# Fox half of the merge inside the front, y splits in the place of u, probabilities divided on ScalarE: a change to a hybrid RWKV-7 and forgetting-attention layer

## The chip, the cores and the metric

The kernel runs on one core of one Trainium2 chip. The metric is the device time of one execution in microseconds (us); the median of several executions stands for a kernel. The engines are named as the profile names them: PE (TensorE matmul), PEld (TensorE weight load), DVE (VectorE), ACT (ScalarE), POOL (GpSimd), SP (SyncE, which issues the DMAs).

## What is computed

One layer over 512 tokens and 16 learned ones put before them (528 rows, 1024 channels). In the reference, cut to what matters:

```python
u = rmsnorm(h, norm_mix)
proj = u @ w_in                              # 1024 -> 1792 (rw) + 1544 (fx) + 2048 (gates)
gates = sigmoid(proj[..., C_RW + C_FX:] + b_gate)
y_rw = rwkv7_branch(feat_rw, ...)            # 8 heads of 64: S = S*w + (S a) b + v k ; y = S r ; group norm, bonus, gate
y_fx = fox_branch(feat_fx, ...)              # 8 heads of 64: causal attention, blocks of 128 queries
#   logits = q.k * scale + F_q - F_k,  F = cumsum(log_sigmoid(f));  p = softmax(mask(logits));  p @ v
merged = gates[..., :1024] * (y_rw @ w_out_rw) + gates[..., 1024:] * (y_fx @ w_out_fx)
h = h + merged @ w_o
z = rmsnorm(h, norm_mlp)
h = h + square(relu(z @ w_up)) @ w_down      # 1024 -> 4096 -> 1024
return h[16:]
```

All is float32. A wide matmul is done in three passes: each operand x is split into `hi` (x cast to the narrower format `fp32r`) and `lo = x - hi`, and `hi*hi + hi*lo + lo*hi` is accumulated. The small matmuls of attention and of the recurrence are done on plain float32.

## The kernel before

**The front.** u is made once, with channels on the partitions, as `uhi` and `ulo` in a pool `up`. The input projection runs in 42 blocks of 128 output columns. The first two (for the low-rank decays and the gate) are made while u is made. The other 40 are jobs in a list sorted by rank (`ask`): 12 of Fox attention (rank 2), 12 of the recurrence (rank 1), 16 of the gates (rank 9). The stream `projections` takes them one by one: `fetch` loads two 256 KB pieces of weights, `convert` splits them (cast on ACT, subtraction on POOL, tiles `wraw`, `whi`, `wlo` with four buffers each), and 48 matmuls follow (L500), in two halves of 264 columns, or for gates in one of 512. A gate block is then copied to `gt` by ACT (L520) and written to DRAM as `gates_d[i]`.

Beside it run other streams. `fox_features` normalises q and k and turns v for the four pairs of heads. `attention` makes, for each pair and each of four query blocks, the scores of both heads (`scored`), their transposes (`turned`) and the product with v (`mixed`). `recurrent` makes for each of four pairs of heads the chunk matrices of the RWKV-7 branch (nine chunks of 64: L826 in `scores`), inverts them for two pairs at once (`inverse`), and starts `chain`, nine dependent steps (L964, L970, L982 and on) through which the state goes; after four chunks each, `group_norm` norms the outputs, turns them and writes `y_rw`.

**What sets the order.** TensorE's instructions stand in the order in which the Python streams are advanced. `Turns.run` always advances the stream of the lowest rank whose next step a planner (`Clock`, a model of each engine's times) holds for ready within the `ROOM` of its rank; a stream can also wait for an `Event`. The other engines' instructions are put in order by a scheduler with priorities, which each stream's rank raises (`AHEAD`).

In `scored` the subtraction of the keys' F and the running minimum are one DVE operation over PSUM and the broadcast row `along[e]` (that is -F of the keys); the causal mask comes in by a matmul of the identity with `masks` into the last 128 columns. ACT takes the exponential with its row sum, DVE the reciprocal `rsum`. In `mixed` the transposed probabilities are the weights and 64 columns of v move (L666 for the 16 learned tokens, L668 for the blocks); ACT scales the result by `rsum` into `yn`, TensorE turns it (L674), ACT copies it into `y_fx`.

**The merge.** When all streams are done, y_rw and y_fx are split into `yhi`, `ylo` (L283, L284). Then come eight output blocks m, for each of them two loads of a piece of weights and, for each branch br, 12 matmuls (L1104) beside this work on a gate tile `gl`, of which each branch has two buffers:

```python
nc.sync.dma_start(g, gates_d[8 * br + m])
G.tensor_tensor(g, g, rs[:, NM:], ALU.mult)                       # L1098, POOL
act(g, g, AF.Tanh, bias=..., scale=0.5)                           # L1099, ACT
V.scalar_tensor_tensor(g, g, 1.0, po, ALU.add, ALU.mult)          # L1106, DVE
...
G.tensor_tensor(pp[0], pp[0], pp[1], ALU.add)                     # L1108, POOL
merged = act(mhi[:, m, :], pp[0], AF.Copy, scale=0.5)             # L1109
V.scalar_tensor_tensor(mlo[:, m, :], pp[0], 0.5, mhi..., ...)     # L1110
```

**The rest.** The output projection runs in two halves (L1136 and L1153), into PSUM banks of the pool that the merge uses too. Then come the second norm, its transposes (L1169) into `zhi`, `zlo`, and the MLP (L1187, L1220). `hres` holds x, loaded behind the merge's loads.

Of the kernel before, what the change touches and what calls it, by code (L numbers as in the profile page):

```python
# [27 lines left out]
CDEC = math.exp(-0.5)  # L28

# [154 lines left out]
class Turns:  # L184
# [5 lines left out]
    ROOM = {0: 0.0, 1: 1.0, 2: 1.5, 3: 1.0, 4: 2.5, 8: 0.5}  # L190
# [32 lines left out]
def kernel(ctx, tc, ht, x, win, par, cst, gain, lora, wout, wo, wup, wdn, out, dbg=None):  # L223
# [16 lines left out]
    masks = cp.tile([128, 2, 128], BF16, name="masks")  # L240
# [55 lines left out]

    with ExitStack() as st:
        up = st.enter_context(tc.tile_pool(name="up", bufs=1))
# [8 lines left out]
        uhi = up.tile([128, KB, T], F32R, name="uhi")  # L307
        ulo = up.tile([128, KB, T], F32R, name="ulo")
# [37 lines left out]
        with tc.tile_pool(name="xp", bufs=2) as xp:  # L346
# [9 lines left out]
            for j in range(2):  # L356
                for i, blk in enumerate((B_LORA, B_GD)):
                    w2[i].append(load_h(win[blk][:, 512 * j:512 * j + 512], V, "w", (4, 4, 4)))
                load_x(0, 1 + j)
# [4 lines left out]
            cmask = xp.tile([128, 128], F32, name="cmask", bufs=1)  # L364
# [35 lines left out]
            V.tensor_copy(masks[:, 0, :], ident)  # L400
            V.tensor_copy(masks[:, 1, :], cmask)
# [36 lines left out]
        for t_ in (lhi, llo):  # L438
            ck.w[t_.tensor.name] = [(0, 128, 0, 2 * T, 14.0)]
# [8 lines left out]
        asked = [0]  # L448

# [8 lines left out]
        def fetch(job):  # L458
            raws = []
            for j in range(2):  # L460
                raw = wp.tile([128, 512], F32, name="wraw", bufs=4)
# [4 lines left out]
        def convert(job, raws):  # L466
            w = []
            for raw in raws:
                hi = wp.tile([128, 512], F32R, name="whi", bufs=4)
                lo = wp.tile([128, 512], F32R, name="wlo", bufs=4)  # L470
# [5 lines left out]
        def projections(total):  # L476
            fetched, done = None, 0
            while done < total:
# [5 lines left out]
                while cur is not None:  # L484
# [29 lines left out]
                    cur = nxt  # L514

        def gate_job(i):
            def begin():
                def evac(po, sl):
                    gt = wp.tile([128, S], F32, name="gt", tag="wraw", bufs=4)
                    A.copy(gt, po)  # L520
                    nc.sync.dma_start(gates_d[i], gt)
# [4 lines left out]
        fox_ready = [Event() for i in range(4)]  # L526
        fox_done = [Event() for i in range(4)]
        fox_tiles = {}

        def fox_features():  # L530
            for p in range(4):
                b0 = B_PAIR + 6 * p
                if p > 1:
                    yield fox_done[p - 2]

                def ask_normed(blk, parts, name):
# [15 lines left out]
                    d["in"] = ask(2, blk, begin, parts)  # L552
# [21 lines left out]
                def begin():  # L574
# [6 lines left out]
                    return evac  # L581
                q = yield from normed(dq, SEQ, qg8)
                v_in = ask(2, b0 + 2, begin)
# [18 lines left out]
        def attention():  # L602
            pTm = fp.tile([128, 2, 128], F32, name="pTm")
            G.memset(pTm, 0.0)
            for p in range(4):
# [10 lines left out]
                def scored(i):  # L616

                    n = NM + 128 * (i + 1)
                    parts = [(0, n)] if n <= 512 else [(0, n - 256), (n - 256, n)]
                    yield lambda: max(ck.ready(q, k), banks(2 * len(parts)))  # L620
                    scs = [[], []]
                    for a, b in parts:
                        for e, hs in enumerate(hss):
                            sc = psm("psc")[:, :b - a]
                            mm(sc, q[hs, 128 * i:128 * i + 128], k[hs, a:b], start=True, stop=b < n)
                            scs[e].append((sc, a, b))
                    for e in range(2):
                        mm(scs[e][-1][0][:, b - a - 128:], masks[:, 0, :], masks[:, 1, :], start=False, stop=True)
                    pes, sums = [], []
                    for e in range(2):  # L630
# [9 lines left out]
                        V.reciprocal(rsum, rsum)  # L640
                        pes.append(pe)
                        sums.append(rsum)
                    return pes, sums
# [18 lines left out]
                def mixed(i, pTs, sums):  # L662
                    yield lambda: max(ck.ready(vt, vm, *pTs[0], *pTs[1], *sums), banks(1))
                    py = psm("py")[:, :128]
                    for e, hs in enumerate(hss):
                        mm(py[:, hs], pTs[e][1], vm[:, hs], start=True, stop=False)  # L666
                        for j in range(i + 1):
                            mm(py[:, hs], pTs[e][0][:, j, :], vt[:, j, hs], start=False, stop=j == i)  # L668
                    yn = fp.tile([128, 128], F32, name="yn")
# [633 lines left out]
```

## Time and profile before

| | |
|---|---|
| median of three executions | 930.76 us (929.88 to 933.67) |
| profiled execution: time, and span in the trace | 930.17 us, 928.4 us |
| busy PE, PEld | 883.4 us (95%), 724.3 us (78%) |
| busy DVE, ACT, POOL | 455.9, 446.7, 194.3 us |
| granted TensorE clock, mean | 0.987 |
| moved by DMA | 107.87 MB, mean 116 GB/s |

A busy time is the sum over an engine's instructions in the profiled execution; the engines run beside each other, so that the shares add up to more than the span. "L500" is line 500 of the kernel. In a group's row stand line, engine, operation, output and inputs, the count, then total busy time and the mean of one in ns; behind a further bar is the engine's idle time just before and what ended most of it. `a <- b: t, n, m` in the list of waits says that a's engine stood idle for t us in n waits that b ended, m the longest. A row of the chain that ended last has the start in us, the duration and the operation.

### The profile page before, as it was taken

The page shows a single profiled execution, that of the slowest core. Times are in us where ns is not written, and L with a number is a line of the kernel's source. Part 1 is how long each engine was busy: PE and PEld are TensorE (multiplying, and loading weights), DVE is VectorE, ACT ScalarE, POOL GpSimd, SP SyncE. Part 2 cuts the span into 40 slices and gives each one's busy share as a digit, 9 for nine tenths or more (in the row PEclk, how much of TensorE's full clock was granted, in tenths as well). Part 3 has the DMA queues.
Part 4 walks back from the last instruction along what each step waited for, and adds up shares of the span by engine and source line. Part 5 has one row for each costly group of instructions (what it writes and reads, how often), then busy time and mean ns, then how long its engine had stood idle before and what let it go on. Part 6 is the DMA issues. An engine that isn't in the chain of part 4 may idle for free.

```text
span 928.4 us, 15700 instructions
## 1 busy us (share of the span) xinstructions
PE 883.4 (95%) x6016; PEld 724.3 (78%) x6016; DVE 455.9 (49%) x850; ACT 446.7 (48%) x933; POOL 194.3 (21%) x170
## 2 busy tenths in 40 slices
PE   7899998998999989999989799999999999999998
PEld 6778876985788777867767578988888888888886
DVE  6574747346538653224675755344423244543322
ACT  7758646364666553555564453344322234442221
POOL 1463733324106442212055400000000000000000
PEclk9999999999999999999999899999999999999999
DMA  5245353225653543444374550132333333332331
GB/s 207 72 118 157 100 132 119 92 70 147 173 171 92 134 133 101 118 141 128 101 234 146 173 175 1 49 100 93 100 92 102 95 98 101 92 103 91 123 116 56
DMA packets 86235, 107.87 MB, mean 116 GB/s; under 512 B 21128, under 2 KB 41864, under 8 KB 86160
## 3 DMA queue, kind: packets, MB, share of 16 engines
q1 hardware_dynamic: 86160, 106.87, 37.9%
q8 instruction: 47, 0.77, 0.3%
q14 instruction: 28, 0.23, 0.1%
HBM read 88.87 MB, written 17.97 MB: 115 GB/s over the span
## 4 chain that ended last, share of the span: by engine, by line
PE 43%; POOL 2%; DVE 2%; DMA 2%; issue 1%; ACT 0%; POOLq 0%; DVEq 0%
PE po L1187 19%; PE pd L1220 19%; PE po L1136 2%; PE po L1153 2%; DMA gl<-gd 2%; POOL gl L1108 1%; POOL gl L1098 1%; DVE ylo L284 1%; PE pd L1169 0%; DVE mlo L1110 0%; DVE gl L1106 0%; ACT mhi L1109 0%; DVE we L284 0%; ACT gl L1099 0%; PE po L1104 0%
## 5 line engine op out<-in xcount | busy, mean ns | idle before, releaser
L260 DVE TENSOR_TENSOR wlo<-wraw,whi 128x512 fp32r<-128x512 f32 x152 | 108.4, 715 | 179.4 <-ACT whi L259 177.9
L259 ACT CAST whi<-wraw 128x512 fp32r<-128x512 f32 x152 | 93.9, 620 | 192.9 <-PE pd L1220 109.6
L500 PE MATMUL pj<-uhi,whi 128*128 128x264 f32 (+1 forms) x480 | 167.2, 348 | 3.0 <-ACT vf L579 2.8
L472 POOL TENSOR_TENSOR wlo<-wraw,whi 128x512 fp32r<-128x512 f32 x80 | 111.7, 1402 | 220.1 <-ACT whi L471 191.6
L500 PE MATMUL pj<-uhi,wlo 128*128 128x264 f32 (+1 forms) x480 | 155.6, 324 | 0.0
L500 PE MATMUL pj<-ulo,whi 128*128 128x264 f32 (+1 forms) x480 | 155.2, 323 | 0.0
L500 PEld LDWEIGHTS pj<-uhi,whi 128*128 128x128 f32 x480 | 91.5, 191 | 17.6 <-issue 5.5
L1220 PE MATMUL pd<-whi,fhi 128*128 128x512 f32 x256 | 99.6, 389 | 0.0
L1220 PE MATMUL pd<-wlo,fhi 128*128 128x512 f32 x256 | 99.6, 389 | 0.0
L1220 PE MATMUL pd<-whi,flo 128*128 128x512 f32 x256 | 99.6, 389 | 0.0
L500 PEld LDWEIGHTS pj<-uhi,wlo 128*128 128x128 f32 x480 | 91.2, 190 | 7.5 <-POOL wlo L472 0.2
L1187 PE MATMUL po<-zhi,whi 128*128 128x512 f32 (+1 forms) x248 | 94.8, 382 | 0.0
L1187 PE MATMUL po<-zlo,whi 128*128 128x512 f32 (+1 forms) x248 | 94.8, 382 | 0.0
L1187 PE MATMUL po<-zhi,wlo 128*128 128x512 f32 (+1 forms) x248 | 94.8, 382 | 0.0
L500 PEld LDWEIGHTS pj<-ulo,whi 128*128 128x128 f32 x480 | 91.7, 191 | 4.0
L471 ACT CAST whi<-wraw 128x512 fp32r<-128x512 f32 x80 | 48.9, 617 | 23.8 <-PE pj L500 13.3
L1220 PEld LDWEIGHTS pd<-wlo,fhi 128*128 128x128 f32 x256 | 48.1, 188 | 10.0
L1220 PEld LDWEIGHTS pd<-whi,flo 128*128 128x128 f32 x256 | 48.1, 188 | 9.9
L1220 PEld LDWEIGHTS pd<-whi,fhi 128*128 128x128 f32 x256 | 48.1, 188 | 9.9
L1187 PEld LDWEIGHTS po<-zhi,wlo 128*128 128x128 f32 x248 | 46.6, 188 | 9.1
L1187 PEld LDWEIGHTS po<-zlo,whi 128*128 128x128 f32 x248 | 46.6, 188 | 9.0
L1187 PEld LDWEIGHTS po<-zhi,whi 128*128 128x128 f32 x248 | 46.6, 188 | 8.9
(307 smaller groups left out, 1487.1 us busy)
## 6 DMA issues: line engine op xcount, KB each, us to landing
wraw<-in_win SPq DMA_DIRECT2D x84, 256.0 KB, 2.9
wraw<-in_wup SPq DMA_DIRECT2D x64, 256.0 KB, 2.6
wraw<-in_wdn SPq DMA_DIRECT2D x64, 256.0 KB, 2.6
rec<-rec SPq DMA_DIRECT2D x36, 256.0 KB, 2.9
gd<-gt SPq DMA_DIRECT2D x16, 256.0 KB, 2.1
wraw<-in_wout SPq DMA_DIRECT2D x16, 256.0 KB, 3.1
gl<-gd SPq DMA_DIRECT2D x16, 256.0 KB, 3.0
wraw<-in_wo SPq DMA_DIRECT2D x16, 256.0 KB, 2.9
```

The costliest lines, as they stand in the source:

```text
L259: A.copy(hi, raw)
L260: low.tensor_tensor(lo, raw, hi.bitcast(F32), ALU.subtract)
L284: V.tensor_tensor(lo, x, hi.bitcast(F32), ALU.subtract)
L471: A.copy(hi, raw)
L472: G.tensor_tensor(lo, raw, hi.bitcast(F32), ALU.subtract)
L500: mm(po, a, b[:, k, a0:a1], start=n == 0, stop=n == 23)
L1098: G.tensor_tensor(g, g, rs[:, NM:], ALU.mult)
L1108: G.tensor_tensor(pp[0], pp[0], pp[1], ALU.add)
L1136: mm(pd[i], a[:, k, 128 * i:128 * i + 128], b, start=k == 0 and n == 0, stop=k == 7 and n == 2)
L1153: mm(po, a[:, k, 128 * i:128 * i + 128], b[:, k, :], start=n == 0, stop=n == 23)
L1187: mm(po[:, t0:t1], a, b[:, k, t0:t1], start=n == 0, stop=n == 23)
L1220: mm(pd[i], a[:, b_, 128 * i:128 * i + 128], b, start=b_ == 0 and n == 0, stop=b_ == 15 and n == 2)
```

## The change

- **Attention.** The mask is added to the last 128 columns in use of `along[e]` by POOL, where before a matmul put it into PSUM; the query blocks go 3, 2, 1, 0, since a masked column of a block is not used by the earlier ones. ACT divides the probabilities by their sum ahead of the transposes. In the product v is the weight, the probabilities move, and the result comes out turned: the two heads use the two halves of the array's columns by turns, and the scaling and the transpose of the result are gone.
- **Gates.** The multiplication of a gate block by `rs` goes from the merge to the front (POOL, before the write to DRAM).
- **The merge.** The pool `up` stays open; y's splits take the tags and memory of `uhi` and `ulo` (and later z's do), so they are made when the last projection has read u. A new stream `fox_merged` makes y_fx's splits, the eight Fox blocks of the merge with their gates, and writes the gated products back to `gates_d[8 + m]`. `rw_split` makes y_rw's splits. The loop behind the front then has only the rw blocks, and loads two tiles for each m, the gate and the gated Fox product.
- **Weights.** `wraw` has five buffers, `whi` and `wlo` have six.
- **The recurrence.** The M matrices are made in tiles `Mt` of three chunks, from which six DMAs each time (four to `rec_d`, two into `M`) take what is kept; the two heads share one tile `M`. The bonus is made in place. A pair's keys and values are asked for by events, the inverse is a stream of its own, and the streams' ranks and `ROOM` are others: recurrent 1, attention 2, Fox features 3, where attention was 1, Fox features 2, recurrent 3.

```diff
-    ROOM = {0: 0.0, 1: 1.0, 2: 1.5, 3: 1.0, 4: 2.5, 8: 0.5}
+    ROOM = {0: 0.0, 1: 1.0, 2: 1.0, 3: 1.5, 4: 2.5, 5: 0.0, 6: 0.0, 8: 0.5}
...
-        return [load_h(src[:, 512 * j:512 * j + 512], low[j], "w", (4, 4, 4)) for j in range(2)]
+        return [load_h(src[:, 512 * j:512 * j + 512], low[j], "w", (WR, WH, WH)) for j in range(2)]
...
-                    gt = wp.tile([128, S], F32, name="gt", tag="wraw", bufs=4)
+                    gt = wp.tile([128, S], F32, name="gt", tag="wraw", bufs=WR)
                     A.copy(gt, po)
-                    nc.sync.dma_start(gates_d[i], gt)
+                    def finish():
+                        G.tensor_tensor(gt, gt, rs[:, NM:], ALU.mult)
+                        nc.sync.dma_start(gates_d[i], gt)
+                    return finish
...
+                    for e in range(2):
+                        G.tensor_tensor(along[e][:, n - 128:n], along[e][:, n - 128:n], cmask, ALU.add)
                     yield lambda: max(ck.ready(q, k), banks(2 * len(parts)))
...
-                    for e in range(2):
-                        mm(scs[e][-1][0][:, b - a - 128:], masks[:, 0, :], masks[:, 1, :], start=False, stop=True)
...
                         V.reciprocal(rsum, rsum)
+                        act(pe[:, :n], pe[:, :n], AF.Copy, scale=rsum)
...
-                        mm(py[:, hs], pTs[e][1], vm[:, hs], start=True, stop=False)
-                        for j in range(i + 1):
-                            mm(py[:, hs], pTs[e][0][:, j, :], vt[:, j, hs], start=False, stop=j == i)
-                    yn = fp.tile([128, 128], F32, name="yn")
-                    for e, hs in enumerate(hss):
-                        act(yn[:, hs], py[:, hs], AF.Copy, scale=sums[e])
-                    ...
-                    nc.tensor.transpose(pyT, yn, ident)
-                    A.copy(y_fx[:, p, 128 * i:128 * i + 128], pyT)
+                        mm(py[hs], vm[:, hs], pTs[e][1], start=True, stop=False)
+                    for j in range(i + 1):
+                        for e, hs in enumerate(hss):
+                            mm(py[hs], vt[:, j, hs], pTs[e][0][:, j, :], start=False, stop=j == i)
+                    A.copy(y_fx[:, p, 128 * i:128 * i + 128], py)
...
-                for i in range(4):
+                for i in (3, 2, 1, 0):
...
-                    for e in range(2):
-                        V.tensor_tensor(M[e][:, c0:c0 + 3, :], sps[e][:, :3, :], bc(tmask, 1, 3), ALU.mult)
-                for e, hs in enumerate(hss):
-                    self.save(hss[1 - e], 128 * e, 128 * e + 128, M[e][hss[1 - e]])
-                    self.save(hs, 384, 448, M[e][hs, :, 64:])
+                    for e, hs in enumerate(hss):
+                        Mt = rp.tile([128, 3, 128], F32, name="Mt", bufs=4)
+                        V.tensor_tensor(Mt, sps[e][:, :3, :], bc(tmask, 1, 3), ALU.mult)
+                        nc.sync.dma_start(self.M[hs, c0:c0 + 3, :], Mt[hs, :, :64])
+                        self.save(hss[1 - e], 128 * e, 128 * e + 128, Mt[hss[1 - e]], c0)
+                        self.save(hs, 384, 448, Mt[hs, :, 64:], c0)
...
+        def part(k, c0, c1):
+            split(merge[0][:, k, c0:c1], merge[1][:, k, c0:c1], (y_rw, y_fx)[k // 4][:, k % 4, c0:c1])
+        def fox_merged():
+            yield projected
+            for name in ("uhi", "ulo"):
+                merge.append(up.tile([128, KB, S], F32R, name="y" + name, tag=name))
+            turns.add(5, rw_split())
+            for p in range(4):
+                yield fox_done[p]
+                part(4 + p, 0, S)
+            w = load_h(wout[0][:, 512:], V, "w", (WR, WH, WH))
+            for m in range(KB):
+                cur, w = w, load_h(wout[m + 1][:, 512:], V, "w", (WR, WH, WH)) if m < KB - 1 else None
+                g = fp.tile([128, S], F32, name="gf", tag="qa", bufs=2)
+                nc.sync.dma_start(g, gates_d[8 + m])
+                act(g, g, AF.Tanh, bias=bgh[:, 8 + m:9 + m], scale=0.5)
+                ...
+                    for n, (a, b) in enumerate(passes([x[:, 128 * k:128 * k + 128] for x in cur], merge)):
+                        mm(po, a, b[:, 4 + k, :], start=k == 0 and n == 0, stop=k == 3 and n == 2)
+                V.scalar_tensor_tensor(g, g, 1.0, po, ALU.add, ALU.mult)
+                nc.sync.dma_start(gates_d[8 + m], g)
+        def rw_split():
+            for k in range(2):
+                part(k, 0, S)
+            for i in range(2):
+                yield normalised[1][i]
+                for k in (2, 3):
+                    part(k, 256 * i, 256 * i + 256)
...
+        turns.add(6, fox_merged())
+        turns.add(1, recurrent())
+        turns.add(2, attention())
+        turns.add(3, fox_features())
...
         for m in range(KB):
-            w = load_w(wout[m])
-            ...
+            w = load_h(wout[m][:, :512], V, "w", (WR, WH, WH))
+            g, other = (mp.tile([128, S], F32, name=f"gl{br}", bufs=2) for br in range(2))
+            nc.sync.dma_start(g, gates_d[m])
+            nc.sync.dma_start(other, gates_d[8 + m])
+            act(g, g, AF.Tanh, bias=bgh[:, m:m + 1], scale=0.5)
+            po = ppo()
+            ...
+            V.scalar_tensor_tensor(g, g, 1.0, po, ALU.add, ALU.mult)
+            G.tensor_tensor(g, g, other, ALU.add)
             merged = act(mhi[:, m, :], g, AF.Copy, scale=0.5)
```

More of the change, by code (lines that the diff above doesn't have):

```diff
@@ L1033, in recurrent, with group @@
             pairs = [Pair(p) for p in range(4)]
+            turned_in = Event()
+            turned_in.done = True
+            def group(g, ev):
+                yield from inverse(g, pairs[2 * g:2 * g + 2])
+                turns.add(0, chain(g, pairs[2 * g:2 * g + 2]))
+                ev.done = True
             pairs[0].ask_keys()
@@ L1051, in recurrent @@
                 yield from q.bonus()
-                if p < 3:
-                    pairs[p + 1].ask_values()
+                spent.done = True
                 if j == 1:
-                    if g == 0:
-                        pairs[2].ask_keys()
-                    yield from inverse(g, pairs[p - 1:p + 1])
-                    turns.add(0, chain(g, pairs[p - 1:p + 1]))
+                    turned_in = Event()
+                    turns.add(1, group(g, turned_in))
             yield normalised[1][1]
-        turns.add(3, recurrent())
@@ L1086 @@
         mp = st.enter_context(tc.tile_pool(name="mp", bufs=1))
-        for j, src in enumerate((y_rw, y_fx)):
-            for k in range(4):
-                split(yhi[:, 4 * j + k, :], ylo[:, 4 * j + k, :], src[:, k, :])
         mhi = mp.tile([128, KB, S], F32R, name="mhi")
```

125 lines of the change are left out of this document (61 added, 64 removed).

## The prediction, made before the changed kernel was run

> **What bounds the kernel now.** I read the page's busy table first, then the windows over three stages, then the list of who waited for whom, then the chain that ended last.
>
> ```profile
> PE 883.4 (95%) x6016; PEld 724.3 (78%) x6016; DVE 455.9 (49%) x850; ACT 446.7 (48%) x933; POOL 194.3 (21%) x170
> ```
> ```profile
> 0.00:467.82 467.82, 435.75 (x3992) 355.77 (x3993) 250.40 (x555) 281.31 (x649) 158.42 (x146) 0.99 0.43 126
> 467.82:548.97 81.15, 72.04 (x288) 55.41 (x288) 52.57 (x67) 41.39 (x68) 35.90 (x24) 0.94 0.58 188
> 548.97:928.40 379.43, 375.59 (x1736) 313.11 (x1736) 152.93 (x230) 124.01 (x218) 0.00 (x0) 1.00 0.28 89
> ```
>
> In a windows row stand the stretch, its length, busy time of PE, PEld, DVE, ACT and POOL, the granted clock, the DMA share and GB/s. The stages are the front (to the first matmul of L1104), the merge with the first half of the output projection (to the first of L1153), and the rest. TensorE is the bound everywhere, but in the front a third of its matmuls are short, and 32.07 us are idle. The rest is a wall of matmuls:
>
> ```profile
> 663.58 87.04 PE pd L1220 x384
> ```
>
> That is 226.7 ns for a 512-column matmul. By it the 288 matmuls of the middle stage are 65.3 us of its 81.15. The granted clock of 0.94 takes 4.9 us; the other 11 us are waits, and the chain that ended last shows their cause:
>
> ```profile
> 486.84 3.19 DMA gl<-gd
> ...
> 490.16 1.30 POOL gl L1098
> 491.46 1.71 POOL gl L1108
> ...
> 493.19 0.64 ACT mhi L1109
> ...
> 493.86 0.70 DVE mlo L1110
> ...
> 494.58 3.32 DMA gl<-gd
> ```
>
> From one gate load to the next are 7.74 us, once for each of the eight output blocks m, though TensorE needs 24 x 0.2267 = 5.44 us for one. The gate tiles have two buffers, so a load waits for the subtraction that last read its buffer. TensorE feels it at the end, where L1136 needs the PSUM banks of the last blocks:
>
> ```profile
> PE pch L970 <- DVE Rs L966: 4.4, 1, 4.4
> PE pup L735 <- ACT lhi L283: 2.9, 1, 2.9
> PE pj L500 <- ACT vf L579: 2.8, 1, 2.8
> PE po L1136 <- DVE gl L1106: 2.5, 1, 2.5
> PE po L1104 <- ACT yhi L283: 2.3, 1, 2.3
> ```
>
> **The front, up to its last projection matmul.** Fox attention gets cheaper on TensorE:
>
> ```profile
> 151.49 0.83 PE L668 MATMUL py<-vt,pT 128*128 128x64 f32 x6
> 152.16 0.39 PE L666 MATMUL py<-vm,pTm 128*128 128x64 f32 x2
> 68.61 0.94 PE L826 MATMUL psr<-Lf,BK 64*128 64x128 f32 x12
> 69.47 0.39 PE L500 MATMUL pj<-uhi,whi 128*128 128x264 f32 x1
> 445.62 0.28 PE L628 MATMUL psc<-masks 128*128 128x128 bf16 x2
> 445.71 0.48 PE L500 MATMUL pj<-uhi,whi 128*128 128x512 f32 x1
> ```
>
> From start to start a pass of L668 takes 0.67/6 = 111 ns. There are 224 passes (160 in L668, 64 in L666): 24.9 us. After the change the values are the weights, 64 columns wide, and the two heads use the two column halves of the array by turns, with 128 columns moving. No row has that form; the nearest is L826, two row halves by turns with 128 columns moving: 0.86/12 = 72 ns. That gives 16.1 us, a saving of 8.8. If the halves did not overlap a pass would stay at 111 and save nothing; if it were half of 111, 12.4 us go. I take 8.8, since L826 is the same amount of data through half an array.
>
> [...]
>
> Gone are also 32 mask matmuls at 0.09/2 = 45 ns (1.4 us) and 16 transposes of L674 at about the 111 ns of a pass (1.8 us). In all 12.0 us go. For the masks, POOL adds the mask to 32 pieces of 128 columns, and for the transposes ACT divides the probabilities:
>
> ```profile
> L639 ACT ACTIVATE pe<-pe,nm 128x144 f32<-128x144 f32 (+3 forms) x32 | 18.3, 571 | 19.0 <-DVE nm L636 18.9
> L640 DVE RECIPROCAL rsum<-rsum 128x1 f32<-128x1 f32 x32 | 5.2, 162 | 10.9 <-ACT pe L639 10.6
> ```
>
> The division is 32 x 0.57 us on ACT, which has 281 of 468 us filled in the front, so its load costs nothing; its latency does: reciprocal and division, 0.73 us, now stand between scores and transposes. In the changed program 3.0 us or more of other matmuls stand between the two in each of the 16 steps (more than 6 in eight of them), and a step needs about 1.3 us of subtract-and-minimum, 0.76 of exponential and this 0.73. I book nothing, and keep it as a rival. The additions on POOL lie behind its weight subtractions; I give them the same cover.
>
> Further, the first wait on lhi (2.9) is met 12 projection matmuls of 264 columns later (0.2267 x 264/512 = 0.12 each, 1.4 us saved), the last wait of the front (2.3) goes, and four group-norm steps on TensorE (seven short matmuls of about 0.11, 0.75 us each, 3.0) move behind the last projection. Recurrent pairs go ahead of attention, weights have five and six buffers instead of four, the M tiles go out by 72 small DMAs in place of 16: these move waits about, and I leave the other idle time as it is. So the last projection matmul ends at E = 467.8 - 12.0 - 1.4 - 2.3 - 3.0 = 449.1.
>
> **From E to the second half of the output projection.** Here the work is not hidden as the text of the change has it. The y splits reuse u's buffers, so the first can only be written when the last projection has read u, and in the changed program's order nothing stands on TensorE between that projection and the Fox merge.
>
> ```profile
> 441.38 0.69 DVE L1003 TENSOR_REDUCE st<-y_rw 128x8 f32<-128x512 f32 x1 [0.95 <-ACT y_rw L994]
> 442.73 0.59 ACT L520 COPY gt<-pj 128x512 f32<-128x512 f32 x1 [1.38 <-PE pj L500]
> 443.37 0.65 ACT L1007 ACTIVATE ysq<-y_rw 128x512 f32<-128x512 f32 x1
> 444.16 1.28 ACT L278 ACT_TABLE_LOAD   x1
> 467.15 2.18 ACT L283 CAST yhi<-y_rw 128x512 fp32r<-128x512 f32 x4 [1.12 <-issue]
> 467.80 2.50 DVE L284 TENSOR_TENSOR ylo<-y_rw,yhi 128x512 fp32r<-128x512 f32 x4 [0.73 <-ACT yhi L283]
> 453.80 0.62 ACT L259 CAST whi<-wraw 128x512 fp32r<-128x512 f32 x1
> 467.80:471.20 3.40, 3.38 (x7) 2.44 (x8) 3.40 (x6) 3.40 (x7) 0.75 (x1) 0.51 0.79 230
> ```
>
> ACT's order behind the chain's last step: the square for the group norm (ends about E + 0.6), the last gate's copy 0.59, a table load 1.28, two small steps 0.5, six casts of y at 0.545 = 3.3, one cast of weights 0.6: the first Fox merge matmul starts at E + 7.0. DVE behind it has six subtractions at 0.63 to 0.69, one group-norm step 0.69 and then wlo, ready at E + 8.8, for the third matmul. Behind such a wait the granted clock is about 0.5 for 3.4 us, as the last row shows (L1104 waited 2.3 just before); that costs up to 1.7, of which 0.8 fall on work here, for the wait for wlo takes part of it. The Fox merge is 96 x 0.2267 = 21.8 us and the four group-norm steps 3.0, so TensorE is through at E + 33.7 if nothing stops it.
>
> The first matmul behind it waits for the last Fox gate product, since its bank is that one's. The Fox gates go by a ring of two as well, and their way is longer:
>
> ```profile
> L1099 ACT ACTIVATE gl<-gl,bgh 128x512 f32<-128x512 f32 x16 | 11.6, 723 | 19.6 <-POOL gl L1098 19.6
> L1106 DVE SCALAR_TENSOR_TENSOR gl<-gl,po 128x512 f32<-128x512 f32 x16 | 10.9, 682 | 0.9 <-ACT gl L1099 0.5 <-PE po L1104 0.3
> gd<-gt SPq DMA_DIRECT2D x16, 256.0 KB, 2.1
> hres<-in_x SPq DMA_DIRECT2D x4, 512.0 KB, 8.1
> ```
>
> Product 0.68, write 2.1, load 3.1, tanh 0.72 and hops: 7 to 7.5 us for two blocks. From the first product at E + 12.7 three rounds and the second of the last pair end at about E + 37. The rw gate loads reuse that tile, so they wait for its write (E + 39.4), behind three of the four hres loads (1.5 MB, issued ahead of them and landing in up to 8.1) on the queue: first two loads at E + 43 and 44, products at E + 44.4 and 45.5. In the changed order the rw blocks go in pairs (two tanh, two products, two additions, two casts): load 3.2, tanh 0.72, product 0.68 twice, addition 1.7, cast 0.64, subtraction 0.70 make 8.0 us for two blocks, hence 3.9 for one against 7.74 before, for the multiplication by rs is gone from POOL there. The last product is at E + 45.5 + 3 x 7.9 = E + 69.1, where TensorE could have had it at E + 59. The output projection needs that bank at its fourth matmul group, and has 0.68 + 7 x 2.72 = 19.7 us to go, and 1.8 of half clock behind its wait: E + 90.6.
>
> **The sum.** 449.1 + 90.6 + 379.4 = 919.1 us of span. The profiled run took 930.17 for a span of 928.4, so 1.8 lie around it: **921.0 us**, against 930.17 of that run and 930.76, the median.
>
> **The rivals.** (1) The waits of the front go with the new order: the 4.4 and 2.8 above, and the half clock behind each (1.7), make 10.6 us; the six buffers and the earlier recurrence speak for it, in-order queues against it. 921 - 10.6 = 910. Chance 0.22. (2) No change: the M tiles now go through DMAs, the inverse waits for them on DVE, and the chain's copies are queued behind that wait; ten chain steps that lose 0.9 us each give 9, so 930. The 4.4 us wait of L970 on DVE shows that such queues bite; that there are projections between the steps speaks against it. Should the column halves not overlap, it is 929.8 as well. Chance 0.14. (3) Slower: the division puts TensorE on hold. A transpose that waits for its probabilities holds all that is behind it, projections too. The added latency is 0.73 for each of two heads, and the mask's addition behind a weight subtraction of 1.4 can add as much. It decides from 0.95 us uncovered in each of 16 steps (15 us: 936); at 1.5 it is 921 + 24 = 945. The 3.0 us between the two speak against it, that three of four late steps have under 4.4 for it. If the gate loop kept its 7.74 for one block, the last product would come 22 us later: 943, with the same sign; the order by pairs speaks against that. Chance 0.12 in all. (4) My forecast, 913 to 926: 0.52.
>
> **How the numbers follow.** Something under 0.5% can't be told from no change. Faster (under 926.1) is the forecast and rival 1: 0.74. Same is rival 2: 0.14. Slower is 0.12. The range for 8 in 10 reaches from 905 (rival 1 with a little of the 12.4 us saving) to 934 (rival 2 and the start of rival 3).
>
> **What would show it.** Right: 96 Fox merge matmuls after the last projection, with a wait of about 7 us ahead of them, L668's successor at about 72 ns a pass, the last rw gate product some 69 us behind the last projection, and a rest of 379 us. Wrong: the last projection later than 455 us or sooner than 440, gate products of the rw half over 5 us apart from block to block, or idle TensorE at the transposes of the probabilities of over 10 us in all.

## The result: no faster, 934.16 us, and the profile after

The changed kernel took 934.16 us (median of 20 executions, 929.32 to 937.05) against 931.05 for the kernel before (20, 928.40 to 933.68), a ratio of 1.0032 with a 95% interval of 1.0017 to 1.0046. The forecast was 921.0 (905 to 934). The profiled execution took 933.79 us for a span of 932.0. The page's busy table, then the windows over the front (to the moment when TensorE begins to wait for the first Fox merge matmul), the middle (to the last matmul of the output projection's first half) and the rest:

```profile
PE 876.4 (94%) x5968; PEld 717.4 (77%) x5968; DVE 451.2 (48%) x850; ACT 461.6 (50%) x941; POOL 200.1 (21%) x202
```
```profile
0.00:462.16 462.16, 424.73 (x3916) 343.17 (x3916) 245.07 (x538) 288.57 (x639) 187.76 (x193) 0.96 0.43 126
462.16:552.50 90.34, 76.02 (x317) 61.16 (x317) 53.52 (x83) 49.55 (x87) 12.32 (x9) 0.91 0.71 233
552.50:932.00 379.50, 375.67 (x1738) 313.09 (x1736) 152.58 (x230) 123.52 (x218) 0.00 (x0) 1.00 0.27 89
```

Counted to the first matmul of the second half, at 552.7, the middle is 90.6 us long. It and the rest are as forecast (90.6 and 379.4). The front should have ended at 449.1 and ended at 462.2. TensorE is busy 11 us less in it, but the granted clock fell from 0.99 to 0.96. Who waited for whom on TensorE, after:

```profile
PE pj L1103 <- ACT whi L261: 6.3, 1, 6.3
PE pch L990 <- ACT uv L980: 5.7, 6, 2.0
PE psc L637 <- DVE pT L667: 5.5, 1, 5.5
PE psc L637 <- DVE ka L575: 5.4, 1, 5.4
...
PE pj L500 <- ACT tm L328: 3.2, 4, 1.1
PE po L1151 <- DVE gf L1104: 3.0, 1, 3.0
```

The waits of 4.4 (L970) and 2.8 (L500 for vf) that stood in the list before are gone, and two of 5.5 us at the attention scores have come. The table splits the front of eight profiled kernels in three: idle (all of TensorE's idle time), half clock (half of the other time in stretches with a granted clock of 0.5: an estimate, by the clock alone; in the changed kernel's trace the 264-column matmuls of L500 start 0.22 us apart at 88 us, with the clock at 0.50, and 0.12 at 83 us, with it at 1.00), and work (what remains). The last two columns are the middle, to the first matmul of the second half, and the start of the recurrence's first chain, by its second group of matmuls.

| kernel | median | front | idle | half clock | work | middle | chain from |
|---|---|---|---|---|---|---|---|
| before | 931.05 | 465.6 | 29.8 | 6.6 | 429.2 | 83.4 | 215.1 |
| changed | 934.16 | 462.2 | 37.4 | 16.7 | 408.0 | 90.6 | 234.7 |
| x1 attention alone | 921.84 | 458.1 | 33.9 | 9.1 | 415.2 | 81.8 | 213.4 |
| x2 x1, rs on POOL in the front | 919.34 | 469.3 | 39.2 | 13.2 | 416.8 | 72.5 | 212.7 |
| x6 x1, rs on DVE in the front | 905.95 | 454.6 | 30.5 | 8.6 | 415.5 | 69.8 | 208.5 |
| x18 x6, new order of streams | 914.49 | 456.2 | 34.1 | 10.5 | 411.6 | 74.4 | 206.5 |
| x17 changed, without M tiles and buffers | 924.52 | 448.3 | 31.4 | 7.3 | 409.6 | 93.1 | 205.9 |
| x19 changed, without buffers | 953.40 | 487.3 | 50.6 | 19.1 | 417.5 | 85.0 | 226.2 |

So the work fell by 21.2 us, and 7.6 of idle time and 10.1 of half clock took most of it back. The 3.4 us that are left in the front are less than the 7.2 by which the middle is longer than before, as forecast.

### The profile page after: what moved, and what is told of

Its sections match the earlier page's. It is cut to its first block, busy times and chain, and to the rows that moved or that the text cites. A ratio compares the mean times of both kernels' runs of the same rounds, so it can differ in the third digit from the quotient of the medians.

```text
span 932.0 us, 15719 instructions
## 1 busy us (share of the span) xinstructions
PE 876.4 (94%) x5968; PEld 717.4 (77%) x5968; DVE 451.2 (48%) x850; ACT 461.6 (50%) x941; POOL 200.1 (21%) x202
## 4 chain that ended last, share of the span: by engine, by line
PE 68%; DVE 9%; ACT 9%; DMA 4%; issue 3%; POOL 3%; SPq 2%; POOLq 0%; ACTq 0%; DVEq 0%
PE po L1232 19%; PE pd L1265 19%; PE pj L500 11%; PE po L1181 3%; PE po L1198 2%; PE pj L1103 2%; DMA wraw<-in_win 2%; PE pw L907 1%; POOL wlo L472 1%; DVE tmp L889 1%; PE po L1151 1%; DVE AX L890 1%; ACT whi L471 1%; PE psc L637 1%; PE pj L390 1%
## 5 line engine op out<-in xcount | busy, mean ns | idle before, releaser
L262 DVE TENSOR_TENSOR wlo<-wraw,whi 128x512 fp32r<-128x512 f32 x152 | 104.3, 691 | 173.8 <-ACT whi L261 171.0
L500 PE MATMUL pj<-uhi,whi 128*128 128x264 f32 (+1 forms) x480 | 168.5, 351 | 3.2 <-ACT tm L328 3.2
L500 PE MATMUL pj<-uhi,wlo 128*128 128x264 f32 (+1 forms) x480 | 157.0, 327 | 0.0
L500 PE MATMUL pj<-ulo,whi 128*128 128x264 f32 (+1 forms) x480 | 157.0, 327 | 0.0
L472 POOL TENSOR_TENSOR wlo<-wraw,whi 128x512 fp32r<-128x512 f32 x80 | 107.7, 1358 | 127.1 <-ACT whi L471 109.4
L500 PEld LDWEIGHTS pj<-uhi,whi 128*128 128x128 f32 x480 | 93.1, 194 | 27.2 <-issue 13.2
L500 PEld LDWEIGHTS pj<-uhi,wlo 128*128 128x128 f32 x480 | 93.0, 194 | 7.2
L500 PEld LDWEIGHTS pj<-ulo,whi 128*128 128x128 f32 x480 | 93.3, 194 | 5.0
L1265 PEld LDWEIGHTS pd<-wlo,fhi 128*128 128x128 f32 x256 | 48.0, 188 | 10.1
```

What stands on the lines that cost most here:

```text
L262: low.tensor_tensor(lo, raw, hi.bitcast(F32), ALU.subtract)
L472: G.tensor_tensor(lo, raw, hi.bitcast(F32), ALU.subtract)
L500: mm(po, a, b[:, k, a0:a1], start=n == 0, stop=n == 23)
L1265: mm(pd[i], a[:, b_, 128 * i:128 * i + 128], b, start=b_ == 0 and n == 0, stop=b_ == 15 and n == 2)
```

## The experiments

Ratios are to the kernel before on the same chip, with the 95% interval.

**Attention alone (x1).** The kernel before with the change's diff from `scored` to the order of the blocks.

> The kernel before, with the attention part of the change alone (mask added to the keys' -F, division on ACT, v as weights in column halves, query blocks 3 to 0). In the changed kernel's trace this part takes 15.1 us off TensorE's own work (py 10.45, masks 2.89, turned results 1.77), while idle time (+7.6) and half clock (+10.1) in the front eat it up. Theory A (the new order of the streams makes those waits, attention is innocent): about 931 - 15 = 916 us, 910 to 922. Rival B (the division's latency or the work added to ACT and POOL makes them): 927 to 934, with idle time in the front over 35 us.

921.84 us, ratio 0.9900 (0.9879 to 0.9921). Work fell by 14.0, as theory A has it, but idle time and half clock rose by 6.6: the projection's waits on ACT grew. Both theories hold part of it.

```profile
PE pj L497 <- ACT vf L576: 4.6, 1, 4.6
PE pj L497 <- ACT gt L517: 3.1, 2, 2.5
```

**The gates' multiplication in the front, on POOL (x2) and on DVE (x6).** x2 is x1 with the change's diff in `gate_job`, and L1098 gone; x6 is x1 with

```diff
-                    A.copy(gt, po)
+                    V.tensor_tensor(gt, po, rs[:, NM:], ALU.mult)
...
-                G.tensor_tensor(g, g, rs[:, NM:], ALU.mult)
```

> The same, and the gates are multiplied by rs in the front, on POOL before they are written, instead of in the merge. The merge's period per output block was 7.74 us, of which this step has 1.30, against 5.44 us of matmuls; without it 6.44. Theory A: 7 periods x 1.30 = 9.1 us less where the loads set the pace, so about 907 to 911, 5 to 9 under the kernel with the attention part alone. Rival B: the multiplications hold up the weight subtractions on POOL in the front, and the gain is under 3 us.

> The kernel before with the attention part, and the gate block times rs made by one DVE operation from PSUM into gt, in place of ACT's copy and POOL's multiplication. With the multiplication on POOL the merge got 10.3 us shorter in the profile (81.8 to 71.5) but the front 11 longer, and the median fell only from 921.8 to 919.3. Theory E (in the front POOL and the fourth weight buffer, which gt shares, were held 1.3 us longer for each gate block): here the front stays as with the attention part alone, the merge is as short: 911 to 916. Rival F (the front's length varies with the order that the planner finds, whatever holds the buffers): 917 to 923.

x2: 919.34 us, 0.9873 (0.9852 to 0.9894), only 2.5 less than x1, which is the small gain that rival B forecast; x6: 905.95 us, 0.9720 (0.9701 to 0.9738). Both merges are shorter, by 9.3 and 12.0 us. With POOL the front gives 11 back, with DVE it doesn't. That fits theory E, and goes beyond its range; but TensorE's written order differs among all three, so that how much of the 13.4 us is POOL's is not separated. The windows of x6, whose merge hardly waits any more (its second half begins at 524.4, 0.9 us behind the end of the second window):

```profile
0.00:454.62 454.62, 424.07 (x3944) 342.09 (x3944) 262.14 (x568) 279.58 (x631) 172.95 (x178) 0.98 0.44 129
454.62:523.50 68.88, 67.88 (x288) 54.93 (x288) 44.85 (x65) 40.49 (x69) 11.64 (x8) 0.98 0.67 217
```

The same step in the changed kernel (x10, the first two lines of the diff, with `finish` reduced to the DMA):

> The changed kernel, with the gate block times rs made by one DVE operation from PSUM in place of ACT's copy and POOL's multiplication. With attention's part alone this step, against the one on POOL, took the front from 469.3 to 454.6 us and the median from 919.3 to 906.0. Theory K (the multiplication on POOL and the longer hold of gt are a main part of the front's new waits here too): front to the last projection and attention 6 to 14 us shorter than 462, 920 to 928. Rival L (the waits here are those of ACT's table loads, the M tiles and the order, gates only fill): 931 to 936.

926.78 us, 0.9959 (0.9942 to 0.9976): 7.4 less than the changed kernel, the front at 454.2. That is what theory K forecast; here too TensorE's written order differs.

**The order of the streams (x3, x18).** x3 gives the changed kernel the old ranks and room; x18 gives x6 the changed kernel's `recurrent`, events, ranks and room.

```diff
-        turns.add(1, recurrent())
-        turns.add(2, attention())
-        turns.add(3, fox_features())
+        turns.add(3, recurrent())
+        turns.add(1, attention())
+        turns.add(2, fox_features())
```

> The changed kernel with the streams' ranks and room as before (attention 1, Fox features 2, recurrent and its inverse 3). Theory A: the two waits of 5.5 us (scores at 118 us behind ACT's table loads, scores at 170 us behind the inverse on DVE) go, with the half clock behind them; the front gets 8 to 17 us shorter: 917 to 926. Rival C (the waits come with the Fox merge, the M tiles' DMAs or the buffers): 931 to 936.

> The kernel with attention's part and rs on DVE (906.0), and the changed kernel's order of streams and requests; M tiles, buffers and merge as before. Theory T (that order has a price of its own where the planner does not have the M tiles to book: in the changed kernel the planner's blindness, which leaves the order alone to act, gave 958.8): 915 to 935. Rival U (the order brings the recurrence forward, as it did beside the M tiles, where it took 11 us off, 937.4 to 926.1): 897 to 906.

x3: 935.74 us, 1.0046 (1.0025 to 1.0068), in rival C's range: the two waits went, but others came, so that the old ranks bring no time back. x18: 914.49 us, 0.9826 (0.9803 to 0.9849), 8.5 more than x6, 0.5 under theory T's range.

**The merge back behind the front (x4).**

```diff
-        turns.add(6, fox_merged())
...
-            w = load_h(wout[m][:, :512], V, "w", (WR, WH, WH))
+            w = load_w(wout[m])
+            for br in range(2): ...   # as before, without the multiplication by rs
```

> The changed kernel with both halves of the merge behind the front again and all y splits there, the gates already multiplied by rs. From the last projection to the second half of the output projection the changed kernel took 90.3 us, the kernel before 83.4. Theory A: 83.4 - 7 x 1.3 = 74.3, and the four group-norm steps (3.0) back ahead of it: 934 - 90.3 + 77.3 = 921, 917 to 925. Rival D (the Fox merge inside the front is worth its place, the front only has other trouble): 934 or more.

926.14 us, 0.9932 (0.9912 to 0.9953). The middle is 74.8, as worked out (74.3), and the front grew by 8.4 instead of 3.0, which puts the time 1.1 us above theory A's range. The Fox half inside the front costs 8.0 us in this kernel, the change of the written order included.

**The two waits at the scores (x7, x8).** Ahead of the scores at 118 us, ACT's rows show six table loads, among which the Ln and Exp of the recurrence and of Fox features stand:

```profile
104.02 1.28 ACT L767 ACT_TABLE_LOAD   x1 [2.70 <-DVE sq L765]
106.25 1.28 ACT L768 ACT_TABLE_LOAD   x1
108.79 1.28 ACT L572 ACT_TABLE_LOAD   x1
110.58 1.28 ACT L750 ACT_TABLE_LOAD   x1
112.85 1.28 ACT L572 ACT_TABLE_LOAD   x1
115.11 1.28 ACT L574 ACT_TABLE_LOAD   x1
...
117.99 1.35 PE L637 MATMUL psc<-ka,qa 64*128 64x272 f32 x4 [5.44 <-DVE ka L575]
```

At 170 us, DVE finishes the inverse and its transposes before it copies pT:

```profile
166.53 1.25 DVE L892 STREAM_TRANSPOSE TT<-AX 128x1024 f32<-128x1024 f32 x1
167.70 1.86 DVE L893 STREAM_TRANSPOSE AX<-AX 128x1024 f32<-128x1024 f32 x1
169.49 0.65 DVE L667 COPY pT<-ppt 128x512 f32<-128x512 f32 x1
...
170.19 1.70 PE L637 MATMUL psc<-ka,qa 64*128 64x400 f32 x4 [5.51 <-DVE pT L667]
```

```diff
-                        V.tensor_copy(pT[:, :i + 1, :]...
+                        (A.copy if p == 0 and i == 3 else V.tensor_copy)(pT[:, :i + 1, :]...   # x7
-                    V.tensor_scalar(sq[:, hc], pq, 1e-24, None, ALU.max)
+                    s_ = V.tensor_scalar(sq[:, hc], pq, 1e-24, None, ALU.max)                  # x8
                 pin = pinned(s_)
```

> The changed kernel, and for the first pair's block of 512 keys ACT instead of DVE copies the transposed probabilities out of PSUM. In the changed kernel the scores at 170 us waited 5.5 us for this copy, which stood behind the inverse's serial steps and two 1.25 to 1.8 us transposes on DVE. If that queue is the cause, the wait shrinks to about 2.5 us and some of the half clock goes: 3 to 6 us less, 928 to 931. Rival G: the scores then wait for the next thing (ACT's table loads stand there too), and the time stays at 933 to 936.

> The changed kernel, and the loading of the joint Ln and Exp table in the recurrent pairs' key norm is bound to the operation just before the Ln, instead of an earlier one, so that tanh can't come between. In the built program 35 table loads become 30, and the five between 104 and 116 us (1.28 us each) one. If they are what the scores at 118 us waited for, that wait of 5.4 falls to under 1 and the half clock behind it goes: 5 to 9 us less, 925 to 929. Rival H: DVE, which has the same pieces in the same stretch, is late by then anyway, and the gain is under 2 us.

x8: 930.98 us, 1.0002 (0.9985 to 1.0019), with TensorE's order unchanged but for two neighbouring pairs of matmuls. The wait for ka is gone, which shows its cause, but only 3.2 us come of it, between what the theory and rival H forecast, and the projection and the scores behind the pT copy wait longer instead:

```profile
PE pj L500 <- ACT tm L328: 8.9, 6, 4.6
PE psc L637 <- DVE pT L667: 6.6, 1, 6.6
```

x7: 945.13 us, 1.0138 (1.0106 to 1.0171). The wait at the scores shrank from 5.5 to 2.4, now for ACT, but the planner, which books the copy on another engine, wrote TensorE another order, and the kernel got 11.0 us slower, outside both ranges. What of that is the order's and what is the load on ACT is not separated. The same pin on x6 (x13):

> The kernel with attention's part and rs on DVE (906.0), with the table load bound to the operation just before the Ln, as in the run that took 3.2 us off the changed kernel. TensorE's order is the same instruction for instruction, the built program has 28 table loads instead of 29. The change can only move ACT's queue: 903 to 907.

906.13 us, 0.9731 (0.9708 to 0.9755): no difference from x6.

**The M tiles and the buffers (x9, x11, x12, x17, x19).** "M tiles" here is `Mt`, its DMAs, the common tile `M` and the bonus in place, all as in the change; no run has the larger buffers without them. x9 is x2 with both, x12 is x6 with both, x11 is x6 with the M tiles alone; x17 is the changed kernel without both, x19 without the buffers (`WR, WH = 4, 4`).

> The kernel with attention part and rs multiplication on POOL in the front (919.3), and beside it the M tiles of three chunks with their 72 DMAs, the bonus in place and five and six weight buffers, but the order of streams and requests as before. The changed kernel with the merge put back (926.1) differs from this only in the streams' order. Theory I (the order costs the 6.8 us): 915 to 921, the buffers may bring something. Rival J (the M tiles' DMAs and waits cost it): 924 to 929.

> The kernel with attention's part and rs on DVE (906.0), and the M tiles of three chunks with their 72 DMAs and the bonus in place; four weight buffers. The same with five and six buffers and rs on POOL cost 18 us (919.3 to 937.4). Theory M (the M tiles' DMAs and the inverse's wait for them cost it): 915 to 926. Rival N (the buffers, which let weight splits run ahead on ACT and POOL of what the recurrence waits for, or the order that the planner then finds, cost it): 903 to 910.

> The same with five buffers for raw weights and six for their halves. Theory M: as the kernel with the M tiles alone, 915 to 926. Rival N: 915 to 926 here and 903 to 910 with the M tiles alone. If both are near 906, the 18 us came from POOL's multiplication together with the buffers, or from the order.

> The changed kernel with the M tiles, their saving and the bonus as before, and, since these take their room, four buffers for the weights; order of streams, attention, POOL's multiplication and the Fox merge as changed. Hiding the M tiles' DMAs from the planner took 31 us off one kernel (948.0 to 916.7) and put 25 on the changed one (934 to 958.8). Theory R (the M tiles' DMAs cost the chip about 11 us wherever they are, the rest is the luck of the order): 918 to 940, with idle and half clock in the front (54 in the changed kernel) still over 40. Rival S (the M tiles are the main loss of the changed kernel too): 900 to 917.

> The changed kernel with four weight buffers of each kind in place of five and six, the M tiles as changed. Without both parts it took 924.5, with both 934. Theory V (the M tiles' part costs, the buffers help or do nothing, as where they took the kernel with the M tiles from 948.0 to 937.5): 933 to 945. Rival W (the buffers cost, the M tiles are free in this order): 922 to 928.

| | without | with M tiles | with M tiles and buffers |
|---|---|---|---|
| on x2 | 919.34 | | x9 937.36, 1.0056 (1.0038 to 1.0074) |
| on x6 | 905.95 | x11 948.01, 1.0180 (1.0152 to 1.0207) | x12 937.52, 1.0074 (1.0051 to 1.0096) |
| changed kernel | x17 924.52, 0.9931 (0.9914 to 0.9949) | x19 953.40, 1.0235 (1.0213 to 1.0257) | 934.16 |

The M tiles cost 42 and 29 us, the buffers give 10 and 19 back. So this part of the change costs, as theories J, M and V have it and rivals I, N and W don't, but more than any of them forecast; that the DMAs and the waits for them are the reason, as J and M say, is not shown by these runs. x17 lies in theory R's range, but its idle time and half clock make 38.7 us, not over 40. Without the two the changed kernel's front has the forecast length:

```profile
0.00:448.32 448.32, 416.90 (x3923) 338.63 (x3923) 249.02 (x542) 290.48 (x645) 188.08 (x193) 0.98 0.43 128
448.32:541.50 93.18, 75.00 (x310) 59.67 (x311) 51.23 (x80) 46.23 (x80) 13.20 (x9) 0.93 0.69 221
```

The chain's second matmuls, from the first to the last start (changed kernel, x17, x19, x11):

```profile
L978 PE MATMUL pch<-Rs,rec x144: 218/218/366, 234.7 to 458.0; 64*64 64x64 f32 x144
```
```profile
L977 PE MATMUL pch<-Rs,rec x144: 216/218/267, 205.9 to 435.0; 64*64 64x64 f32 x144
```
```profile
L978 PE MATMUL pch<-Rs,rec x144: 218/218/267, 226.2 to 450.4; 64*64 64x64 f32 x144
```
```profile
L964 PE MATMUL pch<-Rs,rec x144: 218/289/366, 235.5 to 483.2; 64*64 64x64 f32 x144
```

With the M tiles the chain begins 20 to 29 us later. In x11 it runs 41 us beyond the last projection matmul (442.2), with nothing but its own short matmuls, and then the group norm's, on TensorE, which is idle for 16.8 of 47.8 us there and has half clock all the time:

```profile
445.34:493.13 47.79, 30.98 (x340) 24.85 (x340) 20.07 (x52) 21.10 (x62) 0.00 (x0) 0.50 0.46 139
```

**The M tiles' DMAs, or the order written because of them (x14, x15, x16).** The planner books each DMA on one queue with 2 us to landing. In these runs it skips those that read `Mt`, so that it counts neither their time nor the wait for what they write; all instructions stay.

```diff
-            if not outs:
+            if not outs or (ins and ins[0].tensor.name.startswith("Mt") and str(x.engine).split(".")[-1] == "SP"):
                 continue
```

> The kernel with attention's part, rs on DVE and the M tiles by DMA (948.0), and the planner does not book the DMAs that read Mt; every instruction stays, only the order that the planner writes for TensorE changes, and is then nearly that of the kernel without the M tiles' change (906.0): the second group of key turns stands 3 us of matmuls behind the first instead of 16. In the traces DVE writes the last Mt at 72.6 us with the change and the last M at 72.0 without, so the chip is not held up there. Theory O (the planner's book-keeping of one DMA queue with 2 us to landing makes it place the recurrence later, and its first chain starts 25 us later for it): chain 1 from about 212 instead of 235 us, 906 to 918. Rival P (SP's queue, which the DMAs hold for 11 us for each pair, and the inverse's wait for them on the chip cost it): 930 or more.

> The changed kernel with the same blindness of the planner and nothing else. Theory O: the first chain from about 215 us instead of 235, 8 to 20 us less: 914 to 926. Rival P: 931 to 937. Rival Q (the changed order of the streams has a price of its own, now with less cover at the end): 927 to 931.

> The changed kernel with both: rs on DVE (which alone gave 926.8 against 934) and the blind planner. Theory O: 7 us less than with the blindness alone, 907 to 919. With rival P no less than 925.

x14 (x11 with it): 916.70 us, 0.9858 (0.9840 to 0.9876). 31 of the 42 us are the written order alone (TensorE's and, with it, that of the other engines); the chain begins at 218.3 instead of 235.5. The other 11 are not separated: they can be what this part costs on the chip (DMAs, waits for them, or the bonus in place) or what still differs from x6 in TensorE's order. The three key turns of the first pair, in x11 and in x14:

```profile
72.32 0.89 PE L837 MATMUL pbt<-dg,BK 64*128 64x64 f32 x12
84.30 0.89 PE L837 MATMUL pbt<-dg,BK 64*128 64x64 f32 x12
89.30 0.89 PE L837 MATMUL pbt<-dg,BK 64*128 64x64 f32 x12
```
```profile
72.23 0.89 PE L837 MATMUL pbt<-dg,BK 64*128 64x64 f32 x12
75.44 1.55 PE L837 MATMUL pbt<-dg,BK 64*128 64x64 f32 x24
```

x15 (the changed kernel with it): 958.77 us, 1.0292 (1.0270 to 1.0313); x16 (x10 with it): 953.38 us, 1.0247 (1.0227 to 1.0267). The chain began at 214.4 in x15, as theory O says, and yet the kernel got 25 us slower: idle 47, half clock 18, work 415. x16 is 27 us slower than x10. So in the changed kernel the booking is not what costs: there, theory O falls, and an earlier start of the chain by itself brings nothing. Rivals P and Q forecast far less than the 959 us, too. Why its order does so much worse without the booking is open.

## Why the prediction was wrong, step by step

- **Attention on TensorE: right, and somewhat low.** By the starts of its instructions, waits and half clock taken out, the product fell from 25.4 to 14.9 us (10.45, against 8.8 booked), scores with masks by 2.9 (1.4), and the transposes by 1.8 (1.8). A pass takes 14.9/224 = 67 ns (72 booked). Within a run of 16 it is less: in the row below (1.04 - 0.27)/15 = 51 ns, where 0.27 is the last pass's own length. Against the 111 ns of a pass before, that is less than half inside this run, and 67 ns is 0.6 of it over all 224 passes, with their short runs.

```profile
429.38 1.04 PE L679 MATMUL py<-pT,vt 128*64 128x128 f32 x16
```

- **From the last projection on: right in sum, by luck, since two errors cancel.** 90.6 was forecast and came. The first Fox merge matmul stood at E + 6.3 (7.0), the first Fox product ended at E + 12.8 (12.7), the last at 38.6 (about 37). The first rw product ended 4.2 us late, and one of the rounds took 9.6 instead of 7.9, so that the last came at E + 76.6 instead of 69.1. But the output projection did not wait for it: its last wait was for the sixth product (rows below), at E + 66.8, with 23.7 us left (529.0 to 552.7). There is no wait behind that, though the seventh and eighth products ended at 536.2 and 538.7, so the matmuls that need their banks stand late enough in the written order. I had put 21.5 behind the last one.

```profile
528.29 0.69 DVE L1152 SCALAR_TENSOR_TENSOR gl<-gl,po 128x512 f32<-128x512 f32 x1 [1.72 <-ACT gl L1147]
...
538.02 0.69 DVE L1152 SCALAR_TENSOR_TENSOR gl<-gl,po 128x512 f32<-128x512 f32 x1 [1.87 <-ACT gl L1147]
```
```profile
529.04 0.80 PE L1181 MATMUL po<-whi,mhi 128*128 128x512 f32 x1 [1.21 <-DVE gl L1152]
```

- **The step that failed: "these move waits about, and I leave the other idle time as it is."** It held the M tiles, the buffers and the order at nothing. M tiles and buffers together put 13.9 us on the front (448.3 to 462.2): 6.0 idle and 9.4 half clock, less 1.5 of work. In medians they are 9.6 of the 13.2 us by which the forecast was off (934.2 against 924.5). Without them the same sum is nearly right: E 448.3 for 449.1, span 920.8 for 919.1. That is partly luck: against the kernel before, work fell by 19.6 us where 15.0 were booked, and idle time and half clock rose by 2.3 where 1.4 were to go. The last projection at 462.2 is the one of the forecast's own signs of being wrong (later than 455) that came.
- **Rival 2 named the place and missed the mechanism.** The M tiles do cost the gain. But the chain's steps are no slower (from 234.7 to 295.8 us in the changed kernel, from 205.9 to 269.9 in x17, eight steps each). The chain starts late, but in x15 it starts early and the kernel is slower still. So what makes the idle time and the half clock in the changed kernel, the DMAs on the chip or the order written with them, stays open.
- **Rival 3 stayed out.** Transposes waited 1.6 us in all for divided probabilities, in three waits. In x1 the projection's own waits for ACT's copies grew (4.6 and 3.1 in its list, where before has 2.8). I had said that ACT's load "costs nothing"; that the load and not the new order lengthened them is not shown.
- **Rival 1 came half true**: the 4.4 and 2.8 went, and waits of 5.4 and 5.5 took their place.
- **The additions on POOL** I hid behind weight subtractions, and of rs I counted only what the merge gains. In x10, taking it off POOL is worth 7.4 us.
- **Small misreadings that change nothing above**: over half of the front's matmuls before have 128 moving columns or fewer (2152 of 3992), not a third; 8.1 us to landing is the median of the four hres loads (4.1 to 8.9); 919.1 and 1.8 make 920.9.

A ladder of steps, in medians (each with the order that the planner writes for it): 931.1 before; 921.8 attention; 906.0 rs into the front on DVE; 914.5 new order of streams; 924.5 rs on POOL and the Fox half in the front; 953.4 M tiles; 934.2 larger buffers. The first two rungs alone, x6, are 2.8% faster than before (0.9720, 0.9701 to 0.9738), and beat the changed kernel by 28 us.

## What to carry to other kernels

Where a planner writes one engine's order, an edit's own cost can be summed from rows, but idle time and half clock can't be carried over: over the variants with 407 to 418 us of work in the front they made from 38 us (x13) to 84 (x11), so they belong in the range and not in "as it is". Price the parts that only make room (here tiles emptied by DMAs for the sake of buffers) first, and move a step to an engine that can take it straight from PSUM, in place of a copy, before giving it to one more (x6, where DVE does that with the gates' multiplication, took 905.95 us, and x2, with ACT's copy and POOL's multiplication, 919.34, the written order's share included). To tell an edit from the order it causes, keep every instruction and change only what the planner sees.

## What the runs showed of the hardware

The granted clock halved after a far shorter wait than those of 2.3 us and more behind which I counted it, and the length of a single wait didn't decide. In the changed kernel a wait of 1.1 us (L500, at 85.3 us) was followed by half clock, and one of 2.0 us (L990, at 248.6 us) was not. TensorE's idle time within one step of a grid told more: in the traces of the kernel before and the changed one, every change of the granted clock lies on a grid of 3.41 us. Three such steps, each with the one behind it, had 1.08, 1.50 and 1.88 us without a matmul; half clock followed the first and the third:

```profile
84.26:87.67 3.41, 2.33 (x30) 2.19 (x30) 1.65 (x3) 2.18 (x6) 1.73 (x2) 1.00 0.34 130
87.67:91.08 3.41, 3.41 (x20) 3.21 (x18) 1.07 (x3) 1.22 (x4) 1.24 (x1) 0.50 0.54 174
244.68:248.09 3.41, 1.91 (x30) 1.38 (x28) 0.74 (x2) 1.05 (x2) 2.52 (x3) 1.00 0.86 272
248.09:251.50 3.41, 2.88 (x56) 2.56 (x56) 1.50 (x5) 2.04 (x8) 1.84 (x2) 1.00 0.37 78
278.82:282.23 3.41, 1.53 (x14) 1.17 (x15) 1.11 (x3) 3.35 (x7) 0.14 (x1) 1.00 0.82 222
282.23:285.64 3.41, 3.41 (x33) 2.94 (x32) 1.50 (x4) 2.25 (x8) 1.26 (x1) 0.50 0.55 190
```

The wait of 2.0 us lies across two steps, 1.5 in one and 0.5 in the next. In these two traces, of the steps at full clock that begin behind the first matmul (5.2 us), none of the 491 with under 1.0 us idle was followed by half clock, all 12 with 1.9 us or more were, and of the 12 between, 5 were. Of the steps that begin ahead of it, those of the kernel before from 0.22 and 3.63 us had 3.41 and 2.44 us idle, and the clock stayed at 1.00. In the changed kernel every stretch of half clock that ended within the span lasted 3.41 or 6.83 us; in x11, where TensorE had only the chain's and the group norm's short matmuls, it was at 0.50 over the whole window of 47.8 us shown above.
